# Scan parameters of a hybrid block loaded as rows on ScalarE's queue, and two pairs of scan matrices loaded later

## The chip, the cores and the metric

One Trainium2 chip, one of its cores. The metric is device time in microseconds of one execution of the whole kernel. An engine's queue is its own list of instructions, worked off in order; loads that are issued by SyncE (SP), ScalarE (ACT) or GpSimd (POOL) are then carried out by the 16 DMA engines of the core.

## The reference

The reference is one transformer-like block on x of 1024 tokens by 1024 channels. A vector c gives six modulation vectors, x is normalised and modulated, a mixer follows (a state-space scan on 256 channels, attention on 512, a short convolution on 256), and then a mixture of 16 experts. Cut to what the change touches:

```python
c_act = jax.nn.silu(c)
mod = c_act @ ada_w[l] + ada_b[l]                       # 1024 x 6144
sh1, sc1, g1, sh2, sc2, g2 = jnp.split(mod, 6, axis=-1)
h = modulate(rms_norm(x, norm1_g[l]), sh1, sc1)
proj = h @ w_in                                         # 1024 x 2568: u, q, k, v, f, hc, bg, cg

# s5_mixer: 16 groups of 64 states, 16 channels each
lr = jnp.minimum(lam_re, -1e-4);  li = lam_im           # (16, 64)
dt = jnp.exp(log_dt)[:, None]                           # (16, 1)
mag = jnp.exp(lr * dt)
ab_re, ab_im = mag * jnp.cos(li * dt), mag * jnp.sin(li * dt)
...                                                     # z from ab, lr, li
bb_re = z_re[..., None] * b_re - z_im[..., None] * b_im # ssm_b: (16, 64, 16)
...                                                     # the scan, then ssm_c: (16, 16, 64)
y = y + d_skip * u                                      # ssm_d: (256,)
```

The parameters at stake are small: `lam_re` and `lam_im` have 1024 floats each, `log_dt` has 16, `ssm_d` 256, and `ssm_b_re`, `ssm_b_im`, `ssm_c_re`, `ssm_c_im` have 16384 each.

## The kernel before

The order of all instructions on every engine is that of the program text. The first stage does four things at once for the first 512 tokens: it normalises x (four tiles `xt` of 128 tokens by 1024 channels, 512 KB each), computes the modulation, turns x so that channels lie on partitions, and starts the projections of the convolution.

- SyncE issues, in this order: x tiles 0 to 3 (`load_x`, L292), a 256 KB slice of the weights into `hcs` and one into `zt` (`feed`, L249), four 512 KB pieces of `ada_w` for step 0 (`load_ada`, L303, into `vroom`), two more slices of weights, the four pieces for step 1, then four more slices. The pieces for step 2 and 3 reuse the space of step 0 and 1; x tiles 4 to 7 reuse that of tiles 0 to 3.
- ScalarE issues the load of c (L192) and five loads into `prow` (L195, L197), a tile of 128 by 128 that takes 78 rows of 128 parameters each. Then it loads its table, computes `c_act` (L200), and squares the four x tiles, summing as it goes (`x_sq`, L430).
- TensorE turns `prow` at L469 into `pvp`, and VectorE copies its 78 columns to `pv` (L470). VectorE then waits for the four sums: `x_rs` (L122 and L109 to L114) makes the scales, and L440 applies them to x. TensorE turns x (L445) and, between these, multiplies with `ada_w` (`ada1`, L476).
- A loop over b from 0 to 4 follows (from L529). In each pass it loads, does `ada1(b)`, the sums of the modulation, two pairs of turned and modulated channels blocks (`x_mod`), and matrix products (`groups`, L505 to L508). GpSimd splits the weights that SyncE brought (`feed`, L263, shown as L94) before the loop and in passes 0 to 2.
- GpSimd issues, ahead of its first split, the scan's small parameters: `log_dt` in two loads (L328), `lam_re` and `lam_im` (`ld8`, L323), two loads of ssm_b (L334), four of ssm_c (L337) and `ssm_d` (L339). In `ld8` neighbouring floats of one partition lie 512 bytes apart in memory.
- VectorE uses `lr` at L559 and `ldt` in `vexp` in pass 0, `li` at L974, and `ssm_b` and `ssm_c` in `s5_prep`. Behind the loop GpSimd issues the loads of `q_norm_g` and `k_norm_g` (L719, L720), which VectorE multiplies at L721. It is this instruction that everything later on VectorE stands behind.

The lines of the stage that set its order, shortened:

```python
x_rms(0)                     # L521: four squares on ACT, then the scales on DVE
feed(2, 4)
for k in range(4):
    x_turn(0, k)
    if k == 2:
        ada1(0)
for b in range(5):
    ...
```

Of the kernel before, what the change touches and what calls it, by code (L numbers as in the profile page):

```python
# [8 lines left out]
F32 = mybir.dt.float32  # L9
# [9 lines left out]
P = 128  # L19
# [48 lines left out]
def ap_of(t, off, dims):  # L68
    return bass.AP(tensor=t.tensor, offset=t.offset + off, ap=[list(d) for d in dims])
# [11 lines left out]
def _emit(tc, nc, V, A, G, T, I, out, dump, upto, stack):  # L81
# [11 lines left out]
    def tt(o, a, b, op, eng=None):  # L93
        (eng or V).tensor_tensor(o, a, b, op=op)  # L94
# [55 lines left out]
    st = es_st.enter_context(tc.tile_pool(name="st", bufs=4, side="right"))  # L150


    prow = st.tile([P, P], F32, name="prow", bufs=1)
# [35 lines left out]
    NPV = 48 + 8 + 8 + 8 + 6  # L189
# [4 lines left out]
    for nm, n in (("ada_b", 48), ("norm1_g", 8), ("norm2_g", 8), ("out_norm_g", 8)):  # L194
        nc.scalar.dma_start(out=prow[r0:r0 + n, :], in_=I[nm].rearrange("(r c) -> r c", c=P))  # L195
        r0 += n
    nc.scalar.dma_start(out=prow[r0:r0 + 6, :], in_=I["conv_w"].rearrange("w (r c) -> (w r) c", c=P))  # L197
    adabT, n1T, n2T, ogT, cwT = pv[:, 0:48], pv[:, 48:56], pv[:, 56:64], pv[:, 64:72], pv[:, 72:78]
    c_act = cp.tile([P, 8], F32, name="c_act")
    A.activation(c_act, c_in, AF.Silu)  # L200
# [34 lines left out]
    def feed(n, ahead=None):  # L235

        ahead = (FA if "ada2" in X else 3) if ahead is None else ahead
        for _ in range(n + 1):
            while at_w[0] < min(len(parts), at_w[1] + ahead):
                ch, k0 = parts[at_w[0]]  # L240

                if at_w[0] < 8:
                    raw = (hcs, zt)[at_w[0] % 2][:].rearrange("p a b -> p (a b)")[:, k0 * 256:k0 * 256 + 512].rearrange(
                        "p (k c) -> p k c", k=2)
                else:
                    raw = wp.tile([P, 2, 264], F32, name="wr_", tag="wr_", bufs=3)
                c0 = 0
                for o_, m_ in cols_of[ch]:
                    nc.sync.dma_start(out=raw[:, :, c0:c0 + m_], in_=w_in[:, k0:k0 + 2, o_:o_ + m_])  # L249
                    c0 += m_  # L250
                wraws[at_w[0]] = raw, c0
                at_w[0] += 1
            if _ == n or at_w[1] == len(parts):
                return
            ch, k0 = parts[at_w[1]]
            raw, m_ = wraws.pop(at_w[1])
            at_w[1] += 1
            if k0 == 0:
                wt_[ch] = (wp.tile([P, KD, 264], F32R, name="wh_", tag="wh_"),
                           wp.tile([P, KD, 264], F32R, name="wl_", tag="wl_"))  # L260
            hi, lo = (t_[:, k0:k0 + 2, :m_] for t_ in wt_[ch])
            A.activation(hi, raw[:, :, :m_], AF.Copy)
            tt(lo, raw[:, :, :m_], hi.bitcast(F32), ALU.subtract, G)  # L263
# [26 lines left out]
    def load_x(i):  # L290
        xt = st.tile([P, D], F32, name="xt", tag="xt")
        nc.sync.dma_start(out=xt, in_=I["x"][i * P:(i + 1) * P, :])  # L292
        xts.append(xt)
# [3 lines left out]
    def load_ada(b):  # L297

        for n in range(2):
            o_ = (2 * b + n) % 4 * 2048  # L300
            w = vroom[:, o_:o_ + 2048].rearrange("p (t n c) -> p t n c", t=4, n=2)
            for m in range(2):
                nc.sync.dma_start(out=w[:, :, m, :], in_=adaw[:, 4 * n:4 * n + 4, m * D + b * 256:m * D + b * 256 + 256])  # L303
            adt[b, n] = w
# [12 lines left out]
    def small(shape=(P, 8), dt=F32):  # L317
        cnt[0] += 1
        return sm.tile(list(shape), dt, name=f"sm{cnt[0]}")

    def ld8(nm):
        t = small()
        nc.gpsimd.dma_start(out=t, in_=ap_of(I[nm], 0, [[1, P], [P, 8]]))  # L323
        return t

    ldt = small()
    for two in range(2):
        nc.gpsimd.dma_start(out=ldt[64 * two:64 * two + 64, :], in_=ap_of(I["log_dt"], two, [[0, 64], [2, 8]]))  # L328
    lr, li = ld8("lam_re"), ld8("lam_im")
    br_, bi_ = small((P, 8, 16)), small((P, 8, 16))  # L330
    cl = small((P, 2, P))
    dsk = small((16, 16))
    for t_, nm in ((br_, "ssm_b_re"), (bi_, "ssm_b_im")):
        nc.gpsimd.dma_start(out=t_, in_=ap_of(I[nm], 0, [[16, P], [2048, 8], [1, 16]]))  # L334
    for n, nm in enumerate(("ssm_c_re", "ssm_c_im")):
        for two in range(2):
            nc.gpsimd.dma_start(out=cl[:, n, 64 * two:64 * two + 64],  # L337
                                in_=ap_of(I[nm], 1024 * two, [[2048, 8], [64, 16], [1, 64]]))
    nc.gpsimd.dma_start(out=dsk, in_=ap_of(I["ssm_d"], 0, [[1, 16], [16, 16]]))  # L339

    def mul(a, b, shape=(P, 8)):
        o = small(shape)
        tt(o, a, b, ALU.mult)
        return o
# [79 lines left out]
    def x_sq(half, js=range(4)):  # L424
        if js[0] == 0:
            X[half] = st.tile([P, 4], F32, name="ssx", tag="ssx", bufs=2)
        ss = X[half]
        for j in js:
            sq = st.tile([P, D], BF16, name="sqx", tag="sqx", bufs=1)
            A.activation(sq, xts[half * 4 + j], AF.Square, accum_out=ss[:, j:j + 1])  # L430
# [37 lines left out]
    pvp = ps_ms.tile([P, P], F32, name="pvp", tag="ms")  # L468
    T.transpose(pvp, prow, identF)  # L469
    V.tensor_copy(pv, pvp[:, :NPV])  # L470

    def ada1(b):

        pa = ps_tp.tile([P, 512], F32, name="pa1", tag="tp")
        for t in range(8):
            T.matmul(pa[t % 4 * 32:t % 4 * 32 + 32, :], lhsT=cst[:, t, :],  # L476
                     rhs=adt[b, t // 4][:, t % 4].rearrange("p n c -> p (n c)"), start=(t < 4), stop=(t > 3))
        X["pa"] = pa

    def ada_sum(b):  # L480

        ada_sb = st.tile([P, 512], F32, name="ada_sb", tag="h32", bufs=3)
        A.activation(ada_sb, X["pa"], AF.Copy)
        sump = ps_ms.tile([P, 4], F32, name="sump", tag="ms")
        for c in range(4):
            T.matmul(sump[:, c:c + 1], lhsT=ada_sb[:, c * P:(c + 1) * P], rhs=onesF[:, 0:1], start=True, stop=True)
        o_ = slice(2 * b, 2 * b + 2)
        tt(b1T[:, o_], sump[:, 0:2], adabT[:, o_], ALU.add)
        tt(s1T[:, o_], sump[:, 2:4], ada1p[:, o_], ALU.add)
        tt(s1T[:, o_], s1T[:, o_], n1T[:, o_], ALU.mult)  # L490
# [3 lines left out]
    def groups(b, ch, hf):  # L494

        sl = slice(hf * 512, hf * 512 + 512)
        for cc in range(2):
            if b == 0:
                pool, tag = (ps_tp, "tp") if (ch, cc) == ("cg", 1) else (ps_mm, "mm")
                opened[ch, cc] = pool.tile([P, 512], F32, name="pm", tag=tag)  # L500
            pm = opened[ch, cc]
            cs_ = slice(cc * P, cc * P + P)
            wh, wl = wt_[ch]
            for k in (2 * b, 2 * b + 1):
                T.matmul(pm, lhsT=wh[:, k, cs_], rhs=hTh[:, k, sl], start=(k == 0), stop=False)  # L505
                T.matmul(pm, lhsT=wh[:, k, cs_], rhs=hTl[k][:, sl], start=False, stop=False)
            for k in (2 * b, 2 * b + 1):
                T.matmul(pm, lhsT=wl[:, k, cs_], rhs=hTh[:, k, sl], start=False, stop=(k == KD - 1))  # L508
            if b == 3:
                conv_out(ch, cc, hf, opened.pop((ch, cc)))  # L510
# [18 lines left out]
    for b in range(5):  # L529
        if b:  # L530
            if b < 3:
                load_ada(b + 1)
            if b == 1:
                feed(0, 6)
            if b < 4:
                ada1(b)
            groups(b - 1, "hc", 0)
        if b < 4:
            if b == 3:
                for i in range(4, 8):  # L540
                    load_x(i)
                feed(0)
                x_sq(1, (0, 1))
            ada_sum(b)
            if b == 3:
                x_sq(1, (2, 3))
            for k in (2 * b, 2 * b + 1):
                x_mod(0, k)
            if b < 3:
                feed(2, (4, 2, 0)[b])  # L550
        if b < 2:
            for k in (2 * b + 4, 2 * b + 5):
                x_turn(0, k)
        if b == 4:
            x_rs(1)
        if b:
            groups(b - 1, "cg", 0)
        if b == 0:
            V.tensor_scalar(lr, lr, -1e-4, None, op0=ALU.min)  # L559
            dt_ = vexp(ldt)  # L560
        if b == 1:
            mag = vexp(mul(lr, dt_))
# [625 lines left out]
    with ExitStack() as esa:  # L1188
# [244 lines left out]
        for n, (u, kp) in enumerate(steps):  # L1433
# [4 lines left out]
            t = turn(u, kp)  # L1438
# [12 lines left out]
            if 1 in bs:  # L1451
                if not second and 4 * len(qts) == u + 3:
                    load_q(len(qts))
                if u == 12:
# [11 lines left out]
                    for g in saved:  # L1466
                        nc.gpsimd.dma_start(out=o_all[:, g // 2 * 2:g // 2 * 2 + 2, g % 2 * 4:g % 2 * 4 + 4, :],
                                            in_=od[g].rearrange("p (b h d) -> p b h d", b=2, h=4))
# [800 lines left out]
```

## Time and profile before

| | us |
|---|---|
| median of 3 runs | 1122.28 |
| lowest and highest of them | 1121.11, 1126.86 |
| the profiled execution, its own time | 1124.22 |
| its span, from the first to the last instruction | 1122.4 |
| TensorE busy in the span | 1026.0 |
| VectorE, ScalarE, GpSimd busy | 722.0, 526.0, 311.7 |
| mean granted TensorE clock, as a share of full speed | 0.958 |

The profiled execution took 1.94 us more than the median, and 1.8 us of its time lie outside the span. All times in the rows below count from the start of the span. PE is TensorE (PEld its weight loads), DVE is VectorE, ACT ScalarE, POOL GpSimd, SP SyncE. A row that ends in a bracket says how long the engine sat idle before this instruction and what ended that.

### The profile page before, as it was taken

How to read it: one execution, taken by the hardware profiler on the slowest of the kernel's cores; microseconds unless marked ns; L12 is line 12 of the kernel's file. 1: busy time of each engine (PE TensorE's matmuls, PEld its weight loads, DVE VectorE, ACT ScalarE, POOL GpSimd, SP SyncE). 2: the span in 40 equal slices, each digit the busy share in tenths (PEclk: the TensorE clock that was granted, in tenths of full speed). 3: DMA queues.
4: the chain of work that ended last, by engine and by line, in shares of the span. 5: the costliest groups of instructions: out<-in, count | busy, mean ns of one | idle time of the engine just before them, and what ended most of it. 6: DMA issues, size and time to landing. Idle time of an engine off the chain costs nothing. (4 is left out here: it accounts for less than half of the span.)

```text
span 1122.4 us, 18163 instructions
## 1 busy us (share of the span) xinstructions
PE 1026.0 (91%) x6383; PEld 849.1 (76%) x6383; DVE 722.0 (64%) x1564; ACT 526.0 (47%) x1107; POOL 311.7 (28%) x313
## 2 busy tenths in 40 slices
PE   0999899989999999899799994999999999999994
PEld 0578699978887988887688884677777777777773
DVE  2669702583345344687567778796667899789692
ACT  2351111444554555677532321764444676467470
POOL 4215930243321100138222233121422212122130
PEclk9999879989999999899889996799999999999998
DMA  9901103123787343557165733897788799979772
GB/s 190 355 22 39 38 10 78 39 67 110 224 273 255 102 126 105 159 155 230 35 194 188 243 133 107 301 339 244 233 269 281 238 366 357 375 240 353 253 242 41
DMA packets 102366, 213.53 MB, mean 190 GB/s; under 512 B 13998, under 2 KB 37020, under 8 KB 102108
## 3 DMA queue, kind: packets, MB, share of 16 engines
q1 hardware_dynamic: 89744, 170.93, 45.7%
q0 software_dynamic: 11680, 39.55, 13.0%
q10 hardware_dynamic: 828, 1.62, 0.4%
q8 instruction: 62, 1.02, 0.4%
q14 instruction: 52, 0.43, 0.1%
HBM read 184.41 MB, written 27.05 MB: 188 GB/s over the span
## 5 line engine op out<-in xcount | busy, mean ns | idle before, releaser
L94 DVE TENSOR_TENSOR wel<-wer,weh 128x1024 fp32r<-128x1024 f32 x192 | 223.4, 1219 | 2.2 <-ACT weh L1922 1.5
L1922 ACT ACTIVATE weh<-wer 128x1024 fp32r<-128x1024 f32 x192 | 188.9, 1053 | 4.8 <-DVE oh L1931 1.4
L1977 POOL DMA_INDIRECT out_dram<-y,idx x28 | 58.4, 2087 | 227.6 <-DVE y L2042 137.5
L2005 PE MATMUL pg<-weh,xh 128*128 128x512 f32 x256 | 104.7, 409 | 2.0 <-ACT hid L2163 0.7
L2006 PE MATMUL pg<-weh,xl 128*128 128x512 f32 x256 | 103.1, 403 | 0.0
L94 DVE TENSOR_TENSOR pl<-ptp,ph 128x512 fp32r<-128x512 f32 (+1 forms) x80 | 50.3, 636 | 39.5 <-ACT ph L1314 39.2
L2010 PE MATMUL pg<-wel,xh 128*128 128x512 f32 x256 | 66.5, 398 | 0.0
L2005 PEld LDWEIGHTS pg<-weh,xh 128*128 128x128 f32 x256 | 49.1, 192 | 17.9 <-issue 6.1
L1314 ACT ACTIVATE ph<-ptp 128x512 fp32r<-128x512 f32 (+1 forms) x80 | 44.2, 553 | 30.0 <-PE ptp L1309 29.2
L2006 PEld LDWEIGHTS pg<-weh,xl 128*128 128x128 f32 x256 | 49.1, 192 | 11.6 <-DVE xl L94 0.4
L2010 PEld LDWEIGHTS pg<-wel,xh 128*128 128x128 f32 x256 | 47.9, 189 | 11.3
L1296 ACT ACTIVATE lg<-lg,mn 128x128 f32<-128x128 f32 (+3 forms) x64 | 49.5, 774 | 10.6 <-DVE mn L1285 10.5
L1309 PE MATMUL ptp<-identF,lg 128*128 128x128 f32 x288 | 47.9, 285 | 6.2 <-DVE pl L94 6.0
L2032 PE MATMUL pd<-weh,hh 128*128 128x512 f32 x128 | 52.3, 408 | 0.7 <-ACT hh L2024 0.5
L275 PE MATMUL pmw<-woh,yh 128*128 128x512 f32 x128 | 52.7, 411 | 0.0
L277 PE MATMUL pmw<-woh,yl 128*128 128x512 f32 x128 | 51.2, 400 | 0.0
L2033 PE MATMUL pd<-wel,hh 128*128 128x512 f32 x128 | 50.6, 395 | 0.0
L1991 ACT ACTIVATE xh<-ptx 128x512 fp32r<-128x512 f32 x32 | 19.2, 599 | 62.2 <-issue 58.8
L1329 PE MATMUL po<-ph,vs 128*128 128x256 f32 (+1 forms) x160 | 47.1, 316 | 1.2 <-ACT ot L1333 1.0
L1961 POOL DMA_INDIRECT xg<-h2d,idx x16 | 20.7, 1294 | 89.5 <-DVE wgt L1948 62.5
L1330 PE MATMUL po<-pl,vs 128*128 128x256 f32 (+1 forms) x160 | 40.3, 286 | 0.2
L1133 ACT ACTIVATE r<-pm 128x256 f32<-128x256 f32 x32 | 12.3, 384 | 59.7 <-PE pm L280 55.6
(655 smaller groups left out, 2766.2 us busy)
## 6 DMA issues: line engine op xcount, KB each, us to landing
wer<-in_w_up_dram SPq DMA_DIRECT2D x64, 512.0 KB
wer<-in_w_gate_dram SPq DMA_DIRECT2D x63, 512.0 KB
wer<-in_w_down_dram SPq DMA_DIRECT2D x63, 512.0 KB
adw<-in_ada_w_dram SPq DMA_DIRECT2D x32, 512.0 KB
xt<-in_x_dram SPq DMA_DIRECT2D x16, 512.0 KB
vroom<-in_ada_w_dram SPq DMA_DIRECT2D x16, 512.0 KB
qtd<-qe POOLq DMA_DIRECT2D x16, 256.0 KB, 4.1
qt<-qtd SPq DMA_DIRECT2D x16, 256.0 KB
```

What stands on the lines that cost most here:

```text
L94: (eng or V).tensor_tensor(o, a, b, op=op)
L275: T.matmul(o, lhsT=sh(k), rhs=mh(k), start=(k == 0), stop=False)
L277: T.matmul(o, lhsT=sl(k), rhs=mh(k), start=False, stop=False)
L1296: A.activation(lg[:, :w], lg[:, :w], AF.Exp, bias=mn, scale=-1.0, accum_out=l_all[:, qb, h:h + 1])
L1309: T.transpose(pt[:, c0:c0 + P], lgs[u, b][0][:, k0:k0 + P], identF)
L1922: A.activation(hi, raw, AF.Copy)
L1977: G.indirect_dma_start(out=out[:, :], out_offset=bass.IndirectOffsetOnAxis(ap=ix, axis=0), in_=y, in_offset=None, compute_op=ALU.add)
L2005: T.matmul(pg, lhsT=x[0][:, k, :], rhs=hi, start=(k == 0), stop=False)
L2006: T.matmul(pg, lhsT=x[1][:, k, :], rhs=hi, start=False, stop=False)
L2010: T.matmul(pg, lhsT=x[0][:, k, :], rhs=lo, start=False, stop=(k == KD - 1))
L2032: T.matmul(pd, lhsT=h[0][:, k, :], rhs=hi[:, n, :], start=(k == 0), stop=False)
L2033: T.matmul(pd, lhsT=h[0][:, k, :], rhs=lo[:, n, :], start=False, stop=False)
```

## The change

`lam_re`, `lam_im` and `ssm_d` are loaded as rows of `prow` (rows 78 to 109) by three more loads on ScalarE's queue, with contiguous rows of 512 or 64 bytes, and `log_dt` is loaded whole to every partition by a fourth (`ldt16`). The turn of `prow`, which takes all 128 rows already, now turns them too, and five copies on VectorE bring them from `pvp` and `ldt16` to the tiles that the rest of the kernel reads. The five element-wise loads on GpSimd's queue are gone. The six loads of ssm_b and ssm_c stay on GpSimd's queue, but are issued in pass 3 of the loop, behind the splits of passes 0 to 2 and ahead of the loads of `q_norm_g` and `k_norm_g`.

```diff
     nc.scalar.dma_start(out=prow[r0:r0 + 6, :], in_=I["conv_w"].rearrange("w (r c) -> (w r) c", c=P))
+
+    for n, nm in enumerate(("lam_re", "lam_im")):
+        nc.scalar.dma_start(out=prow[NPV + 8 * n:NPV + 8 * n + 8, :], in_=ap_of(I[nm], 0, [[P, 8], [1, P]]))
+    nc.scalar.dma_start(out=prow[NPV + 16:NPV + 32, 0:16], in_=ap_of(I["ssm_d"], 0, [[16, 16], [1, 16]]))
+    ldt16 = st.tile([P, 16], F32, name="ldt16", bufs=1)
+    nc.scalar.dma_start(out=ldt16, in_=ap_of(I["log_dt"], 0, [[0, P], [1, 16]]))
...
-    def ld8(nm):
-        t = small()
-        nc.gpsimd.dma_start(out=t, in_=ap_of(I[nm], 0, [[1, P], [P, 8]]))
-        return t
-
-    ldt = small()
-    for two in range(2):
-        nc.gpsimd.dma_start(out=ldt[64 * two:64 * two + 64, :], in_=ap_of(I["log_dt"], two, [[0, 64], [2, 8]]))
-    lr, li = ld8("lam_re"), ld8("lam_im")
+    ldt, lr, li = small(), small(), small()
     br_, bi_ = small((P, 8, 16)), small((P, 8, 16))
     cl = small((P, 2, P))
     dsk = small((16, 16))
-    for t_, nm in ((br_, "ssm_b_re"), (bi_, "ssm_b_im")):
-        nc.gpsimd.dma_start(out=t_, in_=ap_of(I[nm], 0, [[16, P], [2048, 8], [1, 16]]))
-    for n, nm in enumerate(("ssm_c_re", "ssm_c_im")):
-        for two in range(2):
-            nc.gpsimd.dma_start(out=cl[:, n, 64 * two:64 * two + 64],
-                                in_=ap_of(I[nm], 1024 * two, [[2048, 8], [64, 16], [1, 64]]))
-    nc.gpsimd.dma_start(out=dsk, in_=ap_of(I["ssm_d"], 0, [[1, 16], [16, 16]]))
+
+    def load_bc():
+        for t_, nm in ((br_, "ssm_b_re"), (bi_, "ssm_b_im")):
+            nc.gpsimd.dma_start(out=t_, in_=ap_of(I[nm], 0, [[16, P], [2048, 8], [1, 16]]))
+        for n, nm in enumerate(("ssm_c_re", "ssm_c_im")):
+            for two in range(2):
+                nc.gpsimd.dma_start(out=cl[:, n, 64 * two:64 * two + 64],
+                                    in_=ap_of(I[nm], 1024 * two, [[2048, 8], [64, 16], [1, 64]]))
...
     V.tensor_copy(pv, pvp[:, :NPV])
+    V.tensor_copy(lr, pvp[:, NPV:NPV + 8])
+    V.tensor_copy(li, pvp[:, NPV + 8:NPV + 16])
+    V.tensor_copy(dsk, pvp[0:16, NPV + 16:NPV + 32])
+    for two in range(2):
+        V.tensor_copy(ldt[64 * two:64 * two + 64, :], ldt16[64 * two:64 * two + 64, two:16:2])
...
                 for i in range(4, 8):
                     load_x(i)
                 feed(0)
+                load_bc()
                 x_sq(1, (0, 1))
```

## Rows read from the trace of the kernel before

**Rows 1.** The page: busy tenths in 40 slices of the span, TensorE and DMA.
```profile
PE   0999899989999999899799994999999999999994
...
DMA  9901103123787343557165733897788799979772
```

**Rows 2.** Waits of all engines, 0 to 24 us: total, times, longest.
```profile
DVE rx_m L122 <- ACT sqx L430: 14.9, 1, 14.9
ACT sqx L430 <- DMA xt<-in_x_dram: 12.8, 2, 10.3
```

**Rows 3.** Timeline of ACT, 0 to 75 us: start, length, line, operation.
```profile
0.80 0.41 ACTq L192 DMA_DIRECT2D c_in<-in_c_dram  x1
...
2.97 0.32 ACTq L197 DMA_DIRECT2D prow<-in_conv_w_dram  x1
...
4.73 1.04 ACT L430 ACTIVATE sqx<-xt 128x1024 bf16<-128x1024 f32 x1
...
5.89 1.06 ACT L430 ACTIVATE sqx<-xt 128x1024 bf16<-128x1024 f32 x1
...
20.94 1.06 ACT L430 ACTIVATE sqx<-xt 128x1024 bf16<-128x1024 f32 x1 [2.43 <-DMA xt<-in_x_dram]
```

**Rows 4.** Stretches: length, busy time by engine, clock, DMA share, GB/s.
```profile
2.50:5.20 2.70, 0.00 (x0) 0.00 (x0) 1.52 (x8) 1.87 (x3) 2.70 (x4) 1.00 1.25 363
5.20:11.20 6.00, 0.45 (x1) 0.18 (x1) 0.37 (x2) 1.81 (x4) 4.05 (x7) 1.00 0.83 2
...
24.00:45.00 21.00, 15.94 (x91) 9.36 (x92) 13.42 (x38) 5.32 (x9) 4.61 (x4) 1.00 1.10 349
```

**Rows 5.** DMA queues, 5.2 to 11.2 us: packets, MB, share (q0 GpSimd's, q1 SyncE's).
```profile
q0 software_dynamic: 38, 0.00, 82.4%
q1 hardware_dynamic: 5, 0.01, 0.4%
```

**Rows 6.** Timeline of DVE, 0 to 75 us.
```profile
7.01 0.24 DVE L470 COPY pv<-pvp 128x78 f32<-128x78 f32 x1 [1.69 <-PE pvp L469]
22.12 0.17 DVE L122 TENSOR_SCALAR rx_m<-ssx 128x4 f32<-128x4 f32 x1 [14.87 <-ACT sqx L430]
...
72.42 0.22 DVE L721 SCALAR_TENSOR_TENSOR gq<-gq,gk__610 128x64 f32<-128x64 f32 x1
```

**Rows 7.** Timeline of PE, 0 to 75 us.
```profile
31.50 3.33 PE L476 MATMUL pa<-vroom,cst 128*32 128x512 f32 x16
...
37.47 1.92 PE L476 MATMUL pa<-vroom,cst 128*32 128x512 f32 x16
...
57.17 1.92 PE L476 MATMUL pa<-vroom,cst 128*32 128x512 f32 x16
```

**Rows 8.** Timeline of POOL, 0 to 75 us.
```profile
6.18 0.91 POOL L334 DMA_DIRECT2D sm<-in_ssm_b_re_dram  x1
...
15.94 0.58 POOL L337 DMA_DIRECT2D sm<-in_ssm_c_im_dram  x1 [4.19 <-DMA sm<-in_log_dt_dram]
...
58.36 1.73 POOL L94 TENSOR_TENSOR wl__225<-zt,wh__224 128x512 fp32r<-128x512 f32 x1
60.04 0.59 POOL L719 DMA_DIRECT2D gq<-in_q_norm_g_dram  x1
```

**Rows 9.** DMA issues, whole span: KB each, median us from issue to landing.
```profile
gq<-in_q_norm_g_dram POOLq DMA_DIRECT2D x1, 32.0 KB, 3.1
...
sm<-in_lam_im_dram POOLq DMA_DIRECT2D x1, 4.0 KB, 14.2
```

**Rows 10.** Line L1071, GpSimd's 16 issues of `qtd`: ns min/median/max, first and last start.
```profile
L1071 POOL DMA_DIRECT2D qtd<-qe x16: 542/554/599, 240.4 to 314.0; - x16
```

**Rows 11.** One stretch with two of those issues; columns as in Rows 4 (DVE third).
```profile
245.00:250.00 5.00, 3.24 (x15) 3.24 (x16) 4.85 (x4) 2.65 (x12) 2.51 (x3) 0.60 0.41 136
```

**Rows 12.** Two later stretches; columns as in Rows 4 (PE first, then its clock).
```profile
57.00:112.20 55.20, 54.68 (x262) 42.63 (x261) 43.45 (x148) 21.30 (x34) 18.70 (x28) 1.00 0.12 26
112.20:168.40 56.20, 51.63 (x252) 45.35 (x250) 21.47 (x25) 9.54 (x19) 35.90 (x34) 0.79 0.10 24
```

## The prediction

> **What bounds the kernel now.** I read the 40 slices first. TensorE is busy in every slice but the first, where it does next to nothing while the DMA engines are fully busy [rows 1]. So the kernel is bound by TensorE and what feeds it, except in the first slice (1122.4 / 40 = 28 us), and the change edits that start. The list of waits for that stretch has two long ones: VectorE waits 14.9 us for ScalarE's squares of x, and ScalarE waits 12.8 us for the loads of x [rows 2]. ScalarE's timeline shows that the first two squares ran at 4.73 and 5.89 us without a wait, and the last one at 20.94, when the fourth tile had just landed [rows 3]. The scales start at 22.12, and from there no load appears as a long wait: the chain of scales, turns, modulation and products paces itself [rows 2, 6, 7].
>
> Why did the second half of x come so late? The stretches say it: 363 GB/s from 2.5 to 5.2 us, then 2 GB/s from 5.2 to 11.2, with the DMA engines 83% busy [rows 4]. In those 6 us the queue of GpSimd had 38 packets that took 82.4% of the engines' time and moved nearly no bytes; SyncE's queue, with x in it, had 5 packets and 0.4% [rows 5]. One such packet held an engine for 0.824 x 16 x 6 / 38 = 2.1 us. What GpSimd had issued by then are the loads of `log_dt`, `lam_re` and `lam_im`, whose elements are single floats: 512 + 512 + 1024 + 1024 of them. These are the loads that the change takes off this queue.
>
> **The change part by part.** *Removed: the element-wise loads.* By 5.2 us two x tiles were in; the second square started at 5.89 unhindered [rows 3]. Two tiles of 0.52 MB remain; at the 363 GB/s of the stretch before the stall they take 1.05 / 0.363 = 2.9 us, so the fourth is through at 8.1 and seen by 8.8 (with the 0.7 us between 5.2 and 5.89). At the 349 GB/s of the steady stretch it is 0.1 us later [rows 4]. So x no longer sets the end; ScalarE does.
>
> *Added on ScalarE: four issues ahead of its table load.* Issues there cost 0.32 us (conv_w, few rows) to 0.41 (c, 128 rows) [rows 3]. Three of the first kind and one of the second: 3 x 0.32 + 0.41 = 1.37 us; bounds 4 x 0.32 = 1.3 and 4 x 0.41 = 1.6. The first square moves from 4.73 to 6.1. The four squares then follow at their own pace, 5.89 - 4.73 = 1.16 us each, the last one at 6.1 + 3 x 1.16 = 9.6, behind the 8.8 of its tile. From the last square to the scales it took 22.12 - 20.94 = 1.18 us. So the scales start at 9.6 + 1.2 = 10.8 instead of 22.12: **11.3 us earlier** [rows 3, 6].
>
> *Added on VectorE: five copies.* The `pv` copy took 0.24 us and started at 7.01, that is 3.7 us after the last row's issue ended (2.97 + 0.32 = 3.29) [rows 3, 6]. With the last issue ending at 3.29 + 1.37 = 4.7 this copy starts at 8.4, and with five more like it VectorE is free at 8.4 + 6 x 0.24 = 9.8. That is 1.0 us before the scales can start, so the wait for ScalarE hides it; without that cover it would cost 1.2. No row shows the load of one 64-byte line to 128 partitions. From below it lands with its neighbours and costs nothing. From above I take the slowest landing of the trace, 14.2 us for `lam_im` [rows 9]: 4.7 + 14.2 = 18.9, which would hold VectorE 8.1 us too long and leave a gain of 3.2. I take the lower bound, since ScalarE's parameter rows are of its kind and its queue.
>
> *Does the earlier chain find its weights?* The next to be late would be `ada_w`. SyncE's order is x, 0.52 MB of weights, 2.10 MB for step 0, 0.52, 2.10 for step 1, 1.05, 2.10 for step 2, 0.52, 2.10 for step 3. From 8.1 us at 349 GB/s [rows 4] step 0 is complete at 8.1 + 2.62 / 0.349 = 15.6, step 1 at 23.1, step 3 at 8.1 + 11.0 / 0.349 = 39.6; 0.7 is added for each to be seen. TensorE wants them at 31.50, 37.47 and 57.17 today, so 11.3 earlier at 20.2, 26.2 and 45.9 [rows 7]. All three arrive first; the tightest margin is step 1 with 2.4 us. Stretched over the stage, the loads and the computation move by about the same amount.
>
> *Moved: ssm_b and ssm_c.* Their six loads now stand behind the split that ends at 58.36 + 1.73 = 60.1 [rows 8], so at 48.8 with the shift, where the DMA engines have almost nothing to do (from 57 us on they are 12% busy) [rows 12]. Queued behind them are GpSimd's two loads for L721, and VectorE works in order behind L721, at 72.42 - 11.3 = 61.1 [rows 6]. Six issues at no more than 0.91 us and the two at 0.59 are 6.6 us, plus 3.1 us to landing [rows 8, 9]: 48.8 + 6.6 + 3.1 = 58.5. So 2.6 us remain, and I cost the move at nothing. The split weights that GpSimd makes next come much later. The readers of ssm_b and ssm_c come behind L721.
>
> Is an issue by GpSimd lengthened when VectorE is busy, as it will be here and was not at 6 to 20 us? The 16 issues of `qtd` took 542 to 599 ns [rows 10], two of them in a stretch in which VectorE was busy 4.85 of 5 us [rows 11]. I see no lengthening, and go by that.
>
> A rule of the Trainium skill speaks the other way: the page SBUF — State Buffer, section "A bandwidth-pool intuition that's wrong (but worth ruling out)", says that a GpSimd-issued transfer of about 620 ns took about 3100 ns beside a VectorE copy, because GpSimd could not write the transfer's descriptors. By that page eight issues would be an estimated 25 us, L721 would come some 16 us late, and the sum would turn from 11 us gained to about 4 lost. No run here shows it so far.
>
> *The sum.* 11.3 us off the profiled execution's own time: 1124.22 - 11.3 = 1112.9. That execution lies 1.94 above the median of the runs, so for the median **1111.0**. Everything behind the first stage only starts earlier, as a block; I find no place later in the span with a load that has a fixed date.
>
> **The rivals.**
> 1. *More than that* (1104 to 1109). TensorE ran at 0.79 of full clock from 112 to 168 us, in which it was busy only 51.63 of 56.2 us [rows 12]. A fall to 1.2 GHz of another length there would move up to 0.21 x 56.2 = 11.8 us either way; a few us are plausible.
> 2. *The `ada_w` loads become the bound.* If the loads run at 231 GB/s between small packets instead of 349, step 1 is complete at 8.1 + 5.24 / 0.231 = 30.8, seen at 31.5, 5.3 us late; gain 6.0, time 1116.3. That rate would need small packets like those removed; against it stands the steady 349 as soon as they were gone [rows 4].
> 3. *The moved loads hold up L721.* Today the six issues, with their stalls, took from 6.18 to 16.5, that is 10.3 us [rows 8]. If they stall so again: 48.8 + 10.3 + 1.2 + 3.1 = 63.4, 2.3 us late, gain 9.0. If the two last loads also take 14.2 to land [rows 9], they are 13.4 late and the gain is gone: a loss of 2.1, 1124.4. For it speaks that GpSimd's issues did stall; against it, that the stalls waited for the `log_dt` loads, which are gone [rows 8]. The page's rule above belongs to this case.
> 4. *The change doesn't do what it says*: x was late for a reason of its own. Then nothing moves, 1122. Against it: the 5 packets of SyncE's queue beside 38 slow ones [rows 5].
> 5. *Slower: TensorE's clock.* The stretch from 57 to 112 us runs at full clock with TensorE busy 54.68 of 55.2 us [rows 12]. If the earlier start makes it wait there in pieces and its clock falls to 1.2 GHz for part of it, a mean of 0.79, as in the stretch behind, would cost 11.6 us and eat the gain. It decides for slower (11.3 + 5.6 us lost) where the mean granted clock of these 55 us is under 0.69. For it: in the next stretch, where TensorE does wait, it fell to 0.79. Against: the margins above leave no gap.
>
> **Chances and range.** One half per cent, 5.6 us, is about what a measurement of this kernel can tell from no change. Forecast 0.66, its own range 1107 to 1115 (the ScalarE bounds give 0.3 us; the rest is the spread of the three runs before, 1.2 below their median and 4.6 above). Rival 1: 0.06, 2: 0.08, 3: 0.10 (half of it still faster), 4: 0.06, 5: 0.04. Faster: 0.66 + 0.06 + 0.08 + 0.05 = 0.85; same 0.05 + 0.06 = 0.11; slower 0.04. The range from 1104 to 1119 takes in rivals 1 and 2 and the upper bound of the `log_dt` load (gain 3.2); rivals 4 and 5 and half of 3, 0.15 together, stay out.
>
> **What would show it.** The first and second square near 6.1 and 7.3, the last near 9.6 with no wait for x; the scales near 10.8; no stretch of 2 GB/s; the four products with `ada_w` each 11 us earlier and without a DMA wait; L721 near 61 without a wait. The prediction is wrong if a square still waits for x past 10 us, if the `pv` copies or L721 wait for a DMA, or if the shift, present at 70 us, is gone at 170: then it was lost to the clock or to a new wait between.

## The result, and the profile after

| | before | after |
|---|---|---|
| median, us (lowest to highest of six runs each) | 1122.32 (1121.11 to 1126.86) | 1114.28 (1109.00 to 1118.06) |
| ratio to before, 95% interval | | 0.9927 (0.9904 to 0.9949) |
| the profiled execution, its own time and span | 1124.22, 1122.4 | 1118.06, 1116.3 |

Faster by 8.0 us between the medians (5.7 to 10.8 by the interval), where 11.3 was forecast. The profiled execution of after is the highest of its six, so shifts below are read at places in the trace, not from the two spans. The first slice of the page is where the picture changes (TensorE and DMA, as in [rows 1]):

```profile
PE   2999899989999999998799994999999999999995
...
DMA  9801113114786433557165632896788699979772
```

ScalarE's timeline holds the first surprise (compare [rows 3]):

```profile
2.97 0.32 ACTq L197 DMA_DIRECT2D prow<-in_conv_w_dram  x1
4.51 0.28 ACTq L200 DMA_DIRECT2D prow<-in_lam_re_dram  x1
5.62 0.28 ACTq L200 DMA_DIRECT2D prow<-in_lam_im_dram  x1
5.94 0.32 ACTq L201 DMA_DIRECT2D prow<-in_ssm_d_dram  x1
6.32 0.45 ACTq L203 DMA_DIRECT2D ldt<-in_log_dt_dram  x1
...
8.21 1.04 ACT L429 ACTIVATE sqx<-xt 128x1024 bf16<-128x1024 f32 x1
...
13.06 1.06 ACT L429 ACTIVATE sqx<-xt 128x1024 bf16<-128x1024 f32 x1 [1.37 <-DMA xt<-in_x_dram]
```

The four issues are as short as forecast: 0.28 + 0.28 + 0.32 + 0.45 = 1.33 us. But ScalarE stood still for 1.22 us before the first of them (3.29 to 4.51) and for 0.83 us before the second (4.79 to 5.62): 2.05 us of waits. These and the issues make up nearly all of the 3.48 us by which the squares are late; they start at 8.21 (4.73 before) instead of the forecast 6.1, and the last one waits for x until 13.06. VectorE's timeline (compare [rows 6]):

```profile
10.12 0.24 DVE L469 COPY pv<-pvp 128x78 f32<-128x78 f32 x1 [1.61 <-PE pvp L468]
...
13.18 0.35 DVE L474 COPY sm<-ldt 64x8 f32<-64x8 f32 x2 [2.61 <-DMA ldt<-in_log_dt_dram]
14.24 0.17 DVE L122 TENSOR_SCALAR rx_m<-ssx 128x4 f32<-128x4 f32 x1 [0.72 <-ACT sqx L429]
...
65.05 0.21 DVE L726 SCALAR_TENSOR_TENSOR gq<-gq,gk__615 128x64 f32<-128x64 f32 x1
```

The scales start at 14.24, that is 7.9 us earlier than the 22.12 of [rows 6]. VectorE had waited 2.61 us for the row of `log_dt` but was through at 13.53, 0.7 us before the sums. The last line, L726, is the multiplication that was L721 before; it has no wait, 7.4 us earlier than in [rows 6].

The stretches (length, busy time of TensorE, its weight loads, VectorE, ScalarE and GpSimd, clock, DMA share, GB/s; the first two against [rows 4], the last two, each 7.5 or 7.6 us earlier, against [rows 12]):

```profile
2.50:5.20 2.70, 0.00 (x0) 0.00 (x0) 1.18 (x7) 0.00 (x0) 0.28 (x1) 1.00 0.96 343
5.20:11.20 6.00, 0.44 (x1) 0.18 (x1) 0.63 (x5) 4.33 (x7) 0.00 (x0) 1.00 0.72 212
...
49.50:104.70 55.20, 54.47 (x260) 42.55 (x260) 43.45 (x148) 21.27 (x34) 23.01 (x34) 1.00 0.14 27
104.60:160.80 56.20, 51.58 (x252) 45.29 (x250) 21.52 (x23) 9.30 (x19) 36.12 (x34) 0.79 0.10 24
```

The stretch of 2 GB/s is gone, but the 212 GB/s in its place are below the 349 to 363 that the forecast went by. The later stretches are the old ones moved: TensorE busy 54.47 instead of 54.68 us, then 51.58 instead of 51.63, at the same clocks. TensorE's products with `ada_w` (against [rows 7]) say the same; the first, the second and the fourth come 7.9, 7.6 and 7.6 us earlier, none with a DMA wait:

```profile
23.64 3.58 PE L480 MATMUL pa<-vroom,cst 128*32 128x512 f32 x16
29.86 1.93 PE L480 MATMUL pa<-vroom,cst 128*32 128x512 f32 x16
...
49.56 1.92 PE L480 MATMUL pa<-vroom,cst 128*32 128x512 f32 x16
```

So the gain is made before 14.24 us and carried on as a block through these stretches, and so is the shortfall: 14.24 - 10.8 = 3.4 us at the scales. In the medians it is 11.3 - 8.0 = 3.3, closer than their interval can tell.

The profile doesn't carry the block to its end. GpSimd's issue of `modd` at 340.68 still comes 7.25 us earlier than before (347.93), but two stretches then take longer, one between its issues of `modd` and one between those of `od`; they are, before and after:

```profile
347.93:367.40 19.47, 17.44 (x172) 14.55 (x171) 6.68 (x17) 7.66 (x28) 4.92 (x6) 1.00 0.69 250
402.96:418.94 15.98, 14.86 (x115) 12.98 (x113) 6.67 (x20) 8.24 (x26) 0.60 (x2) 1.00 0.51 149
```

```profile
340.68:361.88 21.20, 18.82 (x171) 15.81 (x170) 6.68 (x17) 7.67 (x28) 4.91 (x6) 0.92 0.63 230
397.11:414.95 17.84, 16.32 (x115) 14.45 (x113) 6.67 (x20) 8.23 (x26) 0.59 (x2) 0.90 0.49 133
```

The granted clock is 0.92 and 0.90 where it was 1.00, so TensorE worked part of them at the lower of its two levels, 1.2 GHz, and 3.6 us are lost: the shift is 4.0 us at 415, and the span ends 6.1 us shorter. TensorE had pauses ahead of the first fall in both kernels (busy 7.97 us from 350 to 360 before, 7.62 from 342 to 352 after), and only after fell. The profile of e11 below, a kernel as slow as before, has the first of these falls too (345.21 to 366.67, 0.92), so they are not shown to come from the change.

GpSimd's timeline shows the moved loads (against [rows 8]):

```profile
52.43 1.14 POOL L334 DMA_DIRECT2D sm<-in_ssm_b_re_dram  x1
...
56.90 0.64 POOL L724 DMA_DIRECT2D gq<-in_q_norm_g_dram  x1
57.47 0.62 POOL L725 DMA_DIRECT2D gk__615<-in_k_norm_g_dram  x1
```

The eight issues took 52.43 to 58.09, that is 5.7 us against the 6.6 allowed. By the figure of the Trainium skill (SBUF — State Buffer, "A bandwidth-pool intuition that's wrong (but worth ruling out)") they would have taken an estimated 25 us; no issue here was longer than 1.14 us, so the trace does not agree for these issues. VectorE was busy only 1.84 of 5.7 us there, so it is a weak test of the case that the page describes.

What did the four loads wait for? The profile gives a hint in the waits of SyncE's queue, 0 to 24 us (total, times, longest), of before and then of after:

```profile
SPq L292 <- DMA c_in<-in_c_dram: 2.9, 1, 2.9
```

```profile
SPq L298 <- DMA xt<-in_x_dram: 4.1, 2, 2.7
```

An issue of x on SyncE waited for the landing of c, which ScalarE had issued; after the change x waits for x. The compiled program explains it. Each load raises a completion counter when it has landed, so that others can wait for it; loads issued by SyncE and by ScalarE take turns on eight such counters, and a load on a counter waits until the earlier load on the same counter has landed. GpSimd's loads have counters of their own. Four more loads on ScalarE change all partners:

```
before:  x tile 2 waits for c         x tile 3 waits for x tile 0
after:   lam_re   waits for c         lam_im   waits for ada_b
         x tile 2 waits for x tile 0  x tile 3 waits for x tile 1
         later pieces of ada_w and weights wait for lam_re, lam_im, ssm_d, log_dt
```

### The profile page after: what moved, and what is told of

Same layout as the page of the kernel before. It is cut to its first block, busy times and chain, and to the rows that moved or that the text cites. A ratio compares the mean times of both kernels' runs of the same rounds, so it can differ in the third digit from the quotient of the medians.

```text
span 1116.3 us, 18167 instructions
## 1 busy us (share of the span) xinstructions
PE 1028.9 (92%) x6383; PEld 851.9 (76%) x6383; DVE 722.7 (65%) x1569; ACT 526.1 (47%) x1107; POOL 306.4 (27%) x308
## 5 line engine op out<-in xcount | busy, mean ns | idle before, releaser
L1982 POOL DMA_INDIRECT out_dram<-y,idx x28 | 63.2, 2258 | 230.2 <-DVE y L2047 137.7
L2015 PEld LDWEIGHTS pg<-wel,xh 128*128 128x128 f32 x256 | 47.6, 188 | 11.2
```

Source lines behind the costliest of these rows:

```text
L1982: G.indirect_dma_start(out=out[:, :], out_offset=bass.IndirectOffsetOnAxis(ap=ix, axis=0), in_=y, in_offset=None, compute_op=ALU.add)
L2015: T.matmul(pg, lhsT=x[0][:, k, :], rhs=lo, start=False, stop=(k == KD - 1))
```

## The experiments

Two theories for the missing 3.4 us (a third, that the end of x is slow by itself, fell with e1). *Counters*: ScalarE's waits and SyncE's new partners delay squares and x. *The log_dt row*: its load, one 64-byte line to 128 partitions, slows the traffic beside it. They are told apart by the place of the loads. "First" and "fourth" below are the starts of the first and the fourth tile's squares, with the wait for x in brackets; "before" is always the kernel before, run on the same chip. The times inside a kernel come from one profile each; those of e1, e5, e6 and e7, where the scales wait for the same things, agree within 0.2 us.

| kernel | first | fourth | scales | median, us | ratio to before |
|---|---|---|---|---|---|
| before | 4.73 | 20.94 (2.43) | 22.12 | | |
| after | 8.21 | 13.06 (1.37) | 14.24 | 1114.28 | 0.9927 (0.9904 to 0.9949) |
| e1_no_params | 4.80 | 9.67 (0.24) | 10.85 | see text | |
| e2_pool_rows | 4.78 | 11.90 (2.16) | 13.08 | 1115.63 | 0.9928 (0.9903 to 0.9953) |
| e3_log_dt_late | 7.64 | 11.27 (0) | 12.45 | 1113.01 | 0.9909 (0.9878 to 0.9940) |
| e4_params_only | 8.41 | 12.09 (0.18) | 13.46 | 1114.79 | 0.9922 (0.9895 to 0.9949) |
| e5_early_free | 4.77 | 9.71 (0.18) | 10.90 | 1110.46 | 0.9881 (0.9863 to 0.9898) |
| e6_one_single_float_load | 4.74 | 9.54 (0.22) | 10.72 | 1106.58, one run | |
| e7_rows_of_own | 4.74 | 9.64 (0.45) | 10.82 | 1109.93, one run | |
| e8_one_line | 4.74 | 11.65 (2.04) | 12.83 | 1112.65, one run | |
| e9_only_log_dt | 4.73 | 11.64 (0.84) | 12.82 | 1117.64 | 0.9935 (0.9911 to 0.9960) |
| e10_old_log_dt_added | 4.75 | 19.85 (10.51) | 21.03 | 1119.33, one run | |
| e11_bc_only | 4.73 | 19.98 (1.32) | 21.16 | 1123.38 | 0.9990 (0.9974 to 1.0005) |
| e12_x_first | 4.84 | 8.73 (0.37) | 10.89 | 1109.69 | 0.9876 (0.9855 to 0.9898) |

**e1_no_params**: after without the four new loads and their copies; the tiles are filled with constants.

```diff
-    V.tensor_copy(lr, pvp[:, NPV:NPV + 8])
+    V.memset(lr, -0.5)
...
+    V.memset(ldt, -4.0)
```

> The changed kernel without its four new loads; lr, li, ldt and dsk are set to constants, so the output is not the reference's. In the profile of the changed kernel the scales start at 14.2 us, where 10.8 was predicted; 3.4 us are missing. Theory A: the four new loads cost them, because loads issued by SyncE and ScalarE take turns on eight completion counters, and each new load makes later ones wait (ScalarE's own issues 2.0 us, the third and fourth x tile for the first and second). Theory B: the one load of log_dt to 128 partitions slows the DMA engines. Theory C: the tail of x is slow by itself. A and B: first square at 4.7, last one at about 8.3 to 9.0, scales at 9.4 to 10.2, kernel 4 to 5 us faster than the changed one. C: fourth tile still at about 13, scales at 14, time as the changed one.

Without the four loads the scales come at 10.85, and the missing 3.4 us are there. That is later than the 9.4 to 10.2 expected, since the third square waited 1.16 us for x; 10.85 is the floor of this stage as long as that wait stays (e12 takes it away). The total of 1140.36 us says nothing: with other values the program did other work (18516 instructions against 18167 in after).

**e2_pool_rows**: the four loads are issued by GpSimd, at the same early place.

```diff
-        nc.scalar.dma_start(out=prow[NPV + 8 * n:NPV + 8 * n + 8, :], in_=ap_of(I[nm], 0, [[P, 8], [1, P]]))
+        nc.gpsimd.dma_start(out=prow[NPV + 8 * n:NPV + 8 * n + 8, :], in_=ap_of(I[nm], 0, [[P, 8], [1, P]]))
...
-    nc.scalar.dma_start(out=ldt16, in_=ap_of(I["log_dt"], 0, [[0, P], [1, 16]]))
+    nc.gpsimd.dma_start(out=ldt16, in_=ap_of(I["log_dt"], 0, [[0, P], [1, 16]]))
```

> The changed kernel with its four new loads issued by GpSimd, which is idle there, instead of ScalarE. They then take no turn on the counters of SyncE's and ScalarE's loads. Theory A (waits on shared counters): first square at 4.7, last one by 9.5, scales at about 10.5, some 3.5 us faster than the changed kernel, 1110 to 1111 in the median. Theory B (the log_dt load itself slows the DMA engines): ScalarE gains its 3.5 us, but x still comes in late, its fourth tile after 11.5, and VectorE still waits for log_dt until about 13; 1 us gained at most. Theory C: as B.

ScalarE is free again (first square 4.78), yet the scales come at 13.08. VectorE had waited for `log_dt` only until 10.56; what was late is x, as a line of ScalarE's timeline shows:

```profile
11.90 1.06 ACT L429 ACTIVATE sqx<-xt 128x1024 bf16<-128x1024 f32 x1 [2.16 <-DMA xt<-in_x_dram]
```

So the counters alone are not the cause; without them 14.24 - 13.08 = 1.2 us are gained.

**e3_log_dt_late**: the other three loads stay on ScalarE, `log_dt` is issued there behind `feed(2, 4)`, and its copies stand ahead of `vexp`.

```diff
-    nc.scalar.dma_start(out=ldt16, in_=ap_of(I["log_dt"], 0, [[0, P], [1, 16]]))
...
     feed(2, 4)
+    nc.scalar.dma_start(out=ldt16, in_=ap_of(I["log_dt"], 0, [[0, P], [1, 16]]))
```

> The changed kernel with the log_dt load issued by ScalarE behind the squares and the first two weight casts, and its two copies on VectorE right ahead of their reader. The other three new loads stay. Theory B: the stretch from 7 to 12 us then has no lull (over 300 GB/s instead of about 200), the fourth tile lands by 10, and the scales start at about 12.4, set by ScalarE whose issues still wait about 1.7 us. Theory A: ScalarE's waits stay and the third and fourth tile are still issued late (near 4.3 and 6); lull in part, scales at 12.5 to 14.

No square waits for x now. ScalarE sets the end, since it still starts late: 7.64 + 3 x 1.16 = 11.1, measured 11.27:

```profile
7.64 1.04 ACT L428 ACTIVATE sqx<-xt 128x1024 bf16<-128x1024 f32 x1
...
11.27 1.06 ACT L428 ACTIVATE sqx<-xt 128x1024 bf16<-128x1024 f32 x1
```

The row of `log_dt` costs 14.24 - 12.45 = 1.8 us: 1.37 are the wait for x that is gone, the rest is ScalarE's, which has one issue less ahead of the squares. SyncE issued the fourth tile at the same place in both (6.11 and 6.05), so it was its transfer that had been slow. The row alone is not the whole either.

**e4_params_only** and **e11_bc_only** take the two parts of the change apart: e4 is after with the six loads of `ssm_b` and `ssm_c` back at the start, e11 is before with only those six moved.

```diff
+    load_bc()
...
                 feed(0)
-                load_bc()
```

> The changed kernel with the six loads of ssm_b and ssm_c back at the start, issued by GpSimd from about 2.7 us; the parameter rows stay as changed. If the single-float loads made nearly all of the lateness, as predicted, these six (0.26 MB in rows of 64 and 256 bytes) cost under 2.5 us: scales by 16.5, time 1114 to 1117. If the six loads have their own part in it, the fourth tile lands after 16 and the gain over the kernel before falls below 5 us.

> The kernel before with only the six loads of ssm_b and ssm_c moved behind the splits of pass 2; all single-float loads stay at the start. If the single-float loads are the cause, the scales start at 20 to 22 as before and the time is within 2 us of the kernel before; if ssm_b and ssm_c had a part in it (their packets took a third of the DMA time from 16 to 20 us), the scales start up to 4 us earlier, at 18.

e4 is as fast as after, e11 as slow as before: the move of `ssm_b` and `ssm_c` is worth nothing that can be measured, and the other part is the gain.

**e5_early_free** does both remedies: the rows of `lam_re`, `lam_im` and `ssm_d` are issued by GpSimd, `log_dt` by GpSimd behind its first two splits, with its copies ahead of `vexp`.

```diff
-    nc.scalar.dma_start(out=ldt16, in_=ap_of(I["log_dt"], 0, [[0, P], [1, 16]]))
...
     feed(2, 4)
+    nc.gpsimd.dma_start(out=ldt16, in_=ap_of(I["log_dt"], 0, [[0, P], [1, 16]]))
...
+            for two in range(2):
+                V.tensor_copy(ldt[64 * two:64 * two + 64, :], ldt16[64 * two:64 * two + 64, two:16:2])
```

> The changed kernel with lam_re, lam_im and ssm_d loaded as the same rows by GpSimd, and log_dt loaded by GpSimd only behind its first two weight splits, copied right ahead of its reader. If the four new loads cost the missing time in two ways, ScalarE's waits at its issues (about 2 us) and the slowing of x by the log_dt load (1 to 2 us), both are gone: first square at 4.8, fourth tile by 10, scales at 10.8 to 11.3, as without any new load; 2 to 3.5 us faster than the changed kernel, 1111 to 1112 in the median, 0.990 of the kernel before. If the rows themselves slow x, the scales stay at 12.5 or later.

The scales come at 10.90, the floor of e1, 11.2 us ahead of before: 1.8 us from `log_dt` (after to e3) and 1.55 us from ScalarE's issues (12.45 to 10.90) make up the missing 3.4. The split depends on the order: by way of e2 it is 1.2 for ScalarE's issues and 2.2 for `log_dt`. The total follows: 1110.46 us, and its interval does not touch that of after. It is 13.5 us under before in the medians (11.5 to 15.4 by the interval), a little more than the scales gained; where the rest comes from is not shown.

**e6, e7, e8 and e10** (one run each) ask what it is in a load that slows x. Each is e5 with one load more, by GpSimd to a spare tile at the start: e6 the old element-wise load of `lam_re` (1024 single floats), e7 128 rows of 64 bytes each from its own address, e8 128 rows of 64 bytes all from the one line of `log_dt`, e10 the two old loads of `log_dt` (1024 single floats, all from that line).

The added lines of e6, e7, e8 and e10, in this order:

```diff
+    nc.gpsimd.dma_start(out=spare, in_=ap_of(I["lam_re"], 0, [[1, P], [P, 8]]))
```

```diff
+    nc.gpsimd.dma_start(out=spare, in_=ap_of(I["ssm_b_re"], 0, [[16, P], [1, 16]]))
```

```diff
+    nc.gpsimd.dma_start(out=spare, in_=ap_of(I["log_dt"], 0, [[0, P], [1, 16]]))
```

```diff
+    for two in range(2):
+        nc.gpsimd.dma_start(out=spare[64 * two:64 * two + 64, :], in_=ap_of(I["log_dt"], two, [[0, 64], [2, 8]]))
```

> The kernel of e5 with one load of lam_re in the old single-float form (1024 floats) added on GpSimd's queue at the start, into a spare tile. If the single-float loads made x late, in proportion to their count, this one of 3.25 such loads (3328 floats, 11.3 us in all) holds the scales up by about 3.4 us against e5, to 14 to 15. If only many of them together, or the waits between them, did it: no later than e5.

> The kernel of e5 with one load of 128 rows of 64 bytes, each from an address of its own (a piece of ssm_b_re), added on GpSimd's queue at the start. If it is small rows as such that slow x in the log_dt load, the scales come 1.5 to 2.5 us later than in e5, as in e2. If it is that all 128 partitions read one and the same 64 bytes, they come as in e5, within 0.5 us.

> The kernel of e5 with the log_dt load to 128 partitions done once more at the start on GpSimd's queue, into a spare tile that nothing waits for. The DMA slowing alone, without VectorE's wait: if reading the same 64 bytes for 128 partitions slows x, the fourth tile lands 1.5 to 2.5 us later than in e5 and the scales start at 12.5 to 13.5. If not, as e5.

> The kernel of e5 with the two old loads of log_dt (1024 single floats, all from the same 64 bytes) added at the start on GpSimd's queue, into a spare tile. The counterpart of e6, where 1024 single floats from places of their own cost nothing. Theory of the prediction: as in e6, under 1 us, or at most the 3.4 us that are this load's share. Theory D: most of the lateness of the kernel before comes back, fourth tile after 16, scales at 17 to 22.

The queues of the DMA engines from 6 to 13 us show it (q0 is GpSimd's, q1 SyncE's, q10 ScalarE's; packets, MB, share of the engines' time), in the order e6, e7, e8, e10:

```profile
q1 hardware_dynamic: 1416, 2.13, 88.0%
q0 software_dynamic: 32, 0.00, 12.0%
```

```profile
q1 hardware_dynamic: 1737, 2.41, 98.9%
q0 software_dynamic: 32, 0.01, 0.5%
```

```profile
q1 hardware_dynamic: 1263, 1.95, 80.5%
q0 software_dynamic: 32, 0.01, 19.3%
```

```profile
q0 software_dynamic: 34, 0.00, 58.1%
q1 hardware_dynamic: 188, 0.68, 25.2%
```

A packet's share times 16 engines times 7 us over the count: e7 0.005 x 112 / 32 = 0.02 us, e8 0.193 x 112 / 32 = 0.7 us. The two loads have the same shape and size and differ only in the address, and the fourth square moves from 9.64 to 11.65. With single floats it is e6 0.12 x 112 / 32 = 0.4 us and e10 0.581 x 112 / 34 = 1.9 us, near the 2.1 that the prediction read for the packets of before [rows 5]. Those are means over all packets. In e6, e7 and e8 half of them are of 4 bytes and 0.01 us, so one that carries data took twice as long: 0.8, 0.03 and 1.3 us. e6 and e10 move the same number of floats, 1024; the first costs the scales nothing (10.72), the second brings nearly all of the old stall back (21.03), as ScalarE's timeline of e10 shows:

```profile
8.19 1.06 ACT L431 ACTIVATE sqx<-xt 128x1024 bf16<-128x1024 f32 x1 [0.52 <-DMA xt<-in_x_dram]
...
19.85 1.06 ACT L431 ACTIVATE sqx<-xt 128x1024 bf16<-128x1024 f32 x1 [10.51 <-DMA xt<-in_x_dram]
```

The Trainium skill (DMA: Bandwidth & Descriptors, "Rules for kernel authors") says that a strided last dimension becomes one descriptor per element. That fits e6's 0.4 us a packet beside e7's 0.02, but it would price e6 and e10 alike; here the measured addresses decide.

That holds at the start of the kernel. The load of `log_dt` that e5 issues later lands beside weights; q0 from 14 to 21 us:

```profile
q0 software_dynamic: 32, 0.01, 0.6%
```

That is 0.006 x 112 / 32 = 0.02 us a packet, for the same 128 reads of the same line. e8, which has this load twice, shows both: 0.7 us a packet from 6 to 13 us, 0.02 from 18 to 21. In e7 the later load took 0.15. And in after, where ScalarE issues the load, the packets of its queue from 6 to 13 us were short, 0.019 x 112 / 207 = 0.01 us:

```profile
q10 hardware_dynamic: 207, 0.02, 1.9%
```

x was late there all the same, so in after no packet of this load kept an engine for long, and how it slowed x there is open.

**e9_only_log_dt**: before, with `log_dt` alone loaded as in e5; `lam_re`, `lam_im`, `ssm_d`, `ssm_b` and `ssm_c` stay as they were.

```diff
-    for two in range(2):
-        nc.gpsimd.dma_start(out=ldt[64 * two:64 * two + 64, :], in_=ap_of(I["log_dt"], two, [[0, 64], [2, 8]]))
...
+    nc.gpsimd.dma_start(out=ldt16, in_=ap_of(I["log_dt"], 0, [[0, P], [1, 16]]))
```

> The kernel before with log_dt alone changed: its two single-float loads go, and one load of 64 bytes to every partition stands on GpSimd's queue behind the first two weight splits, copied right ahead of its reader. lam_re, lam_im and ssm_d (2304 of the 3328 single floats) stay as before, and so do ssm_b and ssm_c at the start. Theory of the prediction (single floats in proportion): 11.3 x 2304 / 3328 = 7.8 us of the lateness stay, scales at 18.6, time 3.5 us under the kernel before. Theory D (reading the one 64-byte line of log_dt over and over is what blocks x): the scales start at 11 to 12.5, time 9.5 to 11 us under the kernel before, as e5.

The scales move from 22.12 to 12.82, that is 9.3 of the 11.2 us that e5 gains there, with this one load changed. The remaining 1.9 us are left for the other loads that stay; which of them was not tested. The total gained 4.5 to 10.0 us by its interval, so how much of the 9.3 reaches the end isn't resolved.

**e12_x_first**: e5 with x's four loads first in the program text, so that none of them waits on a counter, and two of the old rows of `prow` issued by GpSimd instead.

```diff
+    for i in range(4):
+        load_x(i)
...
+        eng = nc.gpsimd if nm == "out_norm_g" else nc.scalar
+        eng.dma_start(out=prow[r0:r0 + n, :], in_=I[nm].rearrange("(r c) -> r c", c=P))
...
-    nc.scalar.dma_start(out=prow[r0:r0 + 6, :], in_=I["conv_w"].rearrange("w (r c) -> (w r) c", c=P))
+    nc.gpsimd.dma_start(out=prow[r0:r0 + 6, :], in_=I["conv_w"].rearrange("w (r c) -> (w r) c", c=P))
```

> The kernel of e5 with the four x tiles issued ahead of everything else in the program text, so that the third and fourth wait for no completion counter, and with the loads of out_norm_g and conv_w moved from ScalarE's to GpSimd's queue. If the shared counters hold x up (in e5 its third tile makes ScalarE wait 1.2 us), the first square starts at about 4.1, the last one at 8.0 to 8.5, and the scales at 9.2 to 9.8 instead of 10.9; time 1 to 1.5 us under e5. If x is bound by the DMA rate alone, they stay at 10.5 to 10.9.

The fourth square starts at 8.73, a full microsecond earlier, but the scales don't move (10.89). A new wait took the place of the old: VectorE stands before the `pv` copy until the rows that GpSimd issued have landed and been turned, as its timeline in e12 shows:

```profile
10.51 0.24 DVE L470 COPY pv<-pvp 128x78 f32<-128x78 f32 x1 [5.37 <-PE pvp L469]
10.89 0.88 DVE L122 TENSOR_SCALAR rx_m<-ssx 128x4 f32<-128x4 f32 x1
```

e5 and e12 are both faster than before and after, and can't be told from each other.

## Why the prediction was right in kind and forecast 3.4 us too much

- **What bounds the kernel: right.** x was late because of GpSimd's parameter loads, and what the first stage gains goes on as a block, in the profile to 340 us. Rivals 2 and 3 (late `ada_w`, a held L721) left no trace, and the clock of rivals 1 and 5 was as before in their stretches, 1.00 and 0.79. That "everything behind the first stage only starts earlier" is not borne out behind 340 us: a lower clock took 3.6 us of the profiled execution there; whether that is chance is open.
- **Its own signs.** Two of the signs that it named for being wrong came: the fourth square waited for x until 13.06, past 10, and the last copies behind `pv`, those of `ldt`, waited for a DMA until 13.18. That the median stayed inside 1107 to 1115, with 0.7 us to spare, is owed to the width of the range and to luck, not to the sum.
- **"Three of the first kind and one of the second ... 1.37 us": the step that failed first, mis-sized.** It measured 3.48 us (4.73 to 8.21). The issues themselves took 1.33; the 2.05 us of waits on completion counters were not in the sum. Undoing both is worth 1.55 us at the scales (e3 to e5).
- **"I take the lower bound" for the load of `log_dt`: the second, mis-sized.** Its landing was seen at 13.18, 6.4 us after its issue ended at 6.77 and between the two ends given, but that cost nothing by itself. What the step didn't ask is what the load does to others while it runs: it slowed x, and that is most of the 1.8 us from after to e3 (1.37 of waiting). With the first, 3.35 of the 3.4 missing.
- **"The fourth is through at 8.1 and seen by 8.8": wrong for this kernel, and right in e12** (8.73), where no x load waits on a counter. In e5, with both remedies, it is 9.71, since the third tile is still issued behind c's landing. So e5's scales at 10.90 agree with the forecast 10.8 by another way than the forecast's: there x sets the end, and not ScalarE.
- **"Whose elements are single floats": half right.** Taking these loads off was the gain, but not because they were single floats as such. e9 and e10 put 9 to 10 of the 11 us on `log_dt`, the one load whose floats all come from a single 64-byte line, and e6 finds no cost at the scales for as many floats from different addresses. The trace of before has it too: 22 of the 38 packets of [rows 5] carry data, all of 128 bytes, the size of `log_dt`'s; those of `lam_re` and `lam_im`, of 256 bytes, begin at 13.02 and took 0.35 us each instead of 3.4.
- **VectorE's copies, the moved loads, `ada_w`: right.** The `pv` copy came at 10.12 instead of 8.4, since the last issue ended 2.1 us late, and stayed hidden with 0.7 us left of the forecast 1.0. The move of `ssm_b` and `ssm_c` is worth nothing, as costed (e4, e11).

Open: why many reads of one line slow everything beside them at the start and not later. At one size, count and place the address decides (e7 and e8, e6 and e10). But only this one line was tried, and the place counts too: issued at 14.40 us in e5, beside weights in packets of 1 KB (x's are of 4 KB), the same load left their rate at 338 to 349 GB/s. Whether the reads queue at the memory, in a DMA engine or elsewhere, and whether it is x beside them or the time that matters, was not tested.

## What to carry to other kernels

When small parameter loads stand beside a stream that the kernel waits for, look at their addresses too: here a value spread over partitions by many reads of the same few bytes cost more than all other small loads together, and next to nothing once it was issued where no one waited. An added load costs its issue time, its landing, what it does to transfers beside it, and the earlier load that it may have to wait for; read the waits of the issuing queues before you cost it at its issue time alone. A wait that is taken away is worth only the distance to the next one, as e12 shows.

## What the runs showed of the hardware that was not expected

- Beside x's loads, 128 reads of one 64-byte line made x 2.0 us late (e8), and 1024 single-float reads of it 10 us (e10); the same numbers of reads from different addresses made it 0 (e7, e6). One packet held a DMA engine for 0.7 and 1.9 us on average, against 0.02 and 0.4.
- The same 128 reads of that line, carried out beside weights at 18 to 21 us, held an engine for 0.02 us a packet in e5 and e8, 0.15 in e7.
- In this program a load on ScalarE's queue can wait, with ScalarE behind it, for the landing of an earlier load on the same completion counter: 1.22 and 0.83 us in the profile after.
